# RWKV-7 steps of a hybrid decoder kernel: other PSUM rooms, other places in TensorE's queue

## The chip, the cores and the metric

The kernel runs on one core of a Trainium2 chip. The metric is device time in microseconds (us) from launch to end; less is better. Engines are named as in the profile: PE is TensorE (PEld its weight loads), DVE is VectorE, ACT is ScalarE, POOL is GpSimd, SP is SyncE, which here only issues DMAs.

## What is computed

Two decoder layers over 512 tokens of width 1024, all in float32. Each layer runs three mixers side by side on `x`, adds them behind sigmoid gates, and ends with a squared-relu MLP:

```python
proj = x @ w_in[l]
z_a, q_b, k_b, v_b, g_b, u_c, gate_logits = jnp.split(proj, PROJ_SPLITS, axis=-1)
y_a = _rwkv7_mixer(_token_shift(z_a, a_shift[l]), ...)
y_b = _retention_mixer(q_b, k_b, v_b, g_b)
y_c = _s5_mixer(u_c, ...)
gate_a, gate_b, gate_c = jnp.split(jax.nn.sigmoid(gate_logits + b_gate[l]), 3, axis=-1)
merged = gate_a * (y_a @ wb_a) + gate_b * (y_b @ wb_b) + gate_c * (y_c @ wb_c)
x = _layer_norm(DN_ALPHA * x + merged @ w_out[l], ...)
x = _layer_norm(DN_ALPHA * x + jnp.square(jax.nn.relu(x @ w_ff1[l])) @ w_ff2[l], ...)
```

The change touches the RWKV-7 mixer (`y_a`), a recurrence over tokens with a 64x64 state per head, which the kernel does in chunks of 64 tokens:

```python
def step(state, inp):
    r_t, w_t, k_t, v_t, na_t, nb_t = inp
    sa = jnp.einsum('bhvk,bhk->bhv', state, na_t)
    state = (state * w_t[:, :, None, :] + sa[..., None] * nb_t[:, :, None, :]
             + v_t[..., None] * k_t[:, :, None, :])
    return state, jnp.einsum('bhvk,bhk->bhv', state, r_t)
```

## The kernel before

A large product is split in three float32r products (`mm3`, L168 to L171: high by high, low by high, high by low), so nearly all of PE's work stands in L169 to L171. Weight blocks come by DMA (`raw`), ACT makes the high part `wh` (L151) and DVE or POOL the low part `wl` (L155); in the part that the change touches it is always DVE. `raw`, `wh` and `wl` have three buffers each.

In each layer this part is the function `weave`. It mixes nine generators into one program. The **filler** is large products: gate tiles (`gates`), the projections of four retention heads (`b_gemm`), the last gate tiles, and then the three branch products (`branch`, in the order S5, retention, RWKV). The **chains** are small steps that depend on one another: one for each of four pairs of RWKV heads (`a_pair`), one for each of four retention heads (`b_head`). A generator yields (work, latency): `weave` advances a clock by the work, and lets the chain go on when the latency has passed on that clock; until then it takes a piece of filler. At the end all PE instructions of the weave are tied into exactly that order. So a latency in a `yield` decides how much filler stands on PE between a step and the step that needs its result. The order on DVE, ACT and SP is set by the framework's scheduler; every engine works its queue in order.

A pair goes through `a_prep` (decays, key norm, the chunk matrices; transpositions at L697, L741, L763, products at L706, L731, L771), `a_inv` (a triangular inverse on POOL, in and out through DRAM), and `a_post`: a first transposition of the inverted blocks on DVE (L814, `T1` from `PD`; the traces name the tile `T`), then block products of the inverse on PE (L823, L830, L844, L854), the products of L867 and L878, the recurrence over eight chunks (L898 and L901 on PE, with the state scaled to `sbd` on DVE at L906 between them), and a tail: ACT copies the output (`oc`, L911), DVE and ACT normalise it (L918 to L925), PE transposes it (L929), and L931 to L935 apply weight, bias and the gate product L934. A retention head has its scores at L1018, its output at L1038, a norm behind it (L1042 to L1053, with a square root on ACT at L1048), and a transposition at L1061; its gates are a tanh at L999 and a product at L1000 that end a gate tile of the filler.

PSUM has eight rooms of 128x512, in four tags of two: `g` (filler), `m`, `p` and `b`. A new tile of a tag waits until the tile two before it has been read. `a_prep` takes `m`. `a_post` gets its rooms from the argument `bank`, which is `self.mps`, so `m` too; only the recurrence's output `po` is in `p`. The recurrence of pair p waits for the one of pair p-1 by the flag `chain`, but the steps ahead of it do not: they run between the recurrence steps of pair p-1.

Of the kernel before, what the change touches and what calls it, by code (L numbers as in the profile page):

```python
# [21 lines left out]
EARLY, HEAD = 8, 18.0  # L22
# [58 lines left out]
class Hybrid:  # L81
# [469 lines left out]
    def weave(self, chains, filler, head):  # L551

        insts = self.nc.cur_bb.bb.instructions
        start = len(insts)
        self.clock, self.flags, self.joined = 0.0, set(), None
        ready = {id(g): head for g in chains}
        waits = {}
        chains = list(chains)  # L560
        while chains:
            for g in chains:
                if waits.get(id(g), self.flags) is not self.flags and waits[id(g)] not in self.flags:
                    continue
                if ready[id(g)] <= self.clock:
                    break
            else:
                g = filler
                if waits.get(id(g), self.flags) is not self.flags and waits[id(g)] not in self.flags:
                    self.clock += 0.5  # L570
                    continue
            r = next(g, None)
            if r is None:
                if g is filler:
                    live = [ready[id(c)] for c in chains if id(c) not in waits or waits[id(c)] in self.flags]
                    self.clock = max(self.clock, min(live))
                else:
                    chains.remove(g)
                continue
            if isinstance(r, str):  # L580
                waits[id(g)] = r
                if g is filler and r not in self.flags:
                    self.clock += 0.5
                continue
            waits.pop(id(g), None)
            self.clock += r[0]
            ready[id(g)] = self.clock + r[1]
        for _ in filler:
            pass
        last = None  # L590
        for ins in list(insts[start:]):
            if ins.engine == mybir.EngineType.PE:
                if last is not None:
                    self.after(ins, last)
                last = ins
# [46 lines left out]
    def a_prep(self, pool, keep, p):  # L642

        nc, par = self.nc, self.par
# [42 lines left out]
        for t in range(4):  # L687
            PE.matmul(ps[:, 2 * t:2 * t + 2], lhsT=kk[:, 128 * t:128 * t + 128], rhs=self.K[:, K_BO:K_BO + 128:64],
                      start=True, stop=True)
        yield 0.4, 8.5  # L690
        ss = self.small([128, 8], "agm", 2)
        V.tensor_scalar(ss, ps[:, 0:8], 1e-24, None, op0=ALU.max)
        self.rsqrt(rn, ss)
# [1 line left out]
        ps = self.mps()  # L695
        for t in range(4):
            PE.transpose(ps[:, 128 * t:128 * t + 128], m[:, 128 * t:128 * t + 128], self.ident)  # L697
        yield 0.45, 9.0
        V.scalar_tensor_tensor(kk, k, col(P_KK), ps, op0=MUL, op1=MUL)
        V.tensor_scalar(m, a, col(P_KA), self.oka[:, p:p + 1], op0=MUL, op1=ADD)  # L700
        V.tensor_tensor(k, k, m, op=MUL)
# [22 lines left out]
        for g in range(2):  # L724
            ps = [self.mps().rearrange("p (c n) -> p c n", c=4) for _ in range(2)]
            for i in range(4):
                c = 2 * i + g
                for h in range(2):
                    rhs = RAV[H[h], c, :].rearrange("p (s i) -> p s i", i=64)
                    rhs = rhs[:, 0:2, :] if h == 0 else rhs[:, 0:3:2, :]  # L730
                    PE.matmul(ps[h][:, i, :].rearrange("p (s i) -> p s i", i=64), lhsT=BK[H[h], c, :], rhs=rhs,  # L731
                              start=True, stop=True)
            for h in range(2):
                for o, dst in ((0, AB[:, h, g:8:2, 64 * g:64 * g + 64]), (64, AA[:, h, g:8:2, :])):
                    V.tensor_tensor(dst, ps[h][:, :, o:o + 64],
                                    self.K[:, K_MA + o:K_MA + o + 64].unsqueeze(1).to_broadcast([128, 4, 64]), op=MUL)
            yield 1.1, 2.4
        ps = [self.mps().rearrange("p (c n) -> p c n", c=8) for _ in range(2)]
        for c in range(8):
            for h in range(2):  # L740
# [1 line left out]
        for h in range(2):  # L742
            S.copy(out=AB[:, h].rearrange("p (t c) n -> p t (c n)", c=2)[:, :, 64:192],
                   in_=ps[h].rearrange("p (t c) n -> p t (c n)", c=2))
        yield 0.7, 0.8
        nsc = self.dram.tile([16, 2, 64, 64], F32, name=self.nm("nsc"))
        for h in range(2):
            for q in range(2):
# [14 lines left out]
                PE.transpose(ps[h][:, c, :], RAV[H[h], c, 64:192], I64[H[h], :])  # L763
        for h in range(2):
            S.copy(out=AVX[:, h], in_=ps[h])
        yield 0.7, 2.5
        ps = self.mps().rearrange("p (c n) -> p c n", c=8)
        for c in range(8):
            for h in range(2):
# [27 lines left out]
    def a_post(self, pool, p, bank):  # L797
        nc, par = self.nc, self.par
# [3 lines left out]
        H = (slice(0, 64), slice(64, 128))  # L802
        I64 = self.K[:, K_I64:K_I64 + 64]
        tsc, AD, AJ, AB, AVX, RT, vb, pc = (self.ah[p][n] for n in ("tsc", "AD", "AJ", "AB", "AVX", "RT", "vb", "pc"))
        v = page("avb")
        nc.sync.dma_start(out=v, in_=vb)
        PD, T1 = page("PD", 1, (128, 8, 32)), page("T1", 1, (128, 8, 32))
# [4 lines left out]
                                  in_=tsc[b, 8 * h:8 * h + 8].rearrange("c j r -> j c r"))  # L812

        V.transpose(T1, PD)  # L814
        if self.joined:
            self.after(self.nc.cur_bb.bb.instructions[-1], self.joined)
        Pt = page("Pt", 1, (128, 8, 64))
        Y = T1
        Q = [slice(32 * b, 32 * b + 32) for b in range(4)]
# [3 lines left out]
                PE.matmul(ps[Q[b], c, :], lhsT=AD[Q[b], c, :], rhs=T1[Q[b], c, :], start=True, stop=True,  # L823
                          tile_position=(32 * b, 32 * b))
        V.tensor_copy(T1, ps[:, 0:8, :])
        yield 0.7, 2.8
        ps = bank().rearrange("p (c n) -> p c n", c=16)
        for c in range(8):
            for b in range(4):
# [43 lines left out]
        for g in range(2):  # L873
            cs4 = slice(4 * g, 4 * g + 4)
            ps = bank().rearrange("p (c n) -> p c n", c=4)
            for i in range(4):
                for h in range(2):
                    PE.matmul(ps[H[h], i, :], lhsT=WM[H[h], 4 * g + i, :], rhs=AB[H[h], h, 4 * g + i, :],  # L878
                              start=True, stop=True)

            blocks = lambda t: t.rearrange("p (t c) (s n) -> p t (c s) n", c=2, n=64)
            V.tensor_tensor(blocks(GM[:, cs4])[:, :, 0:4:3], blocks(ps)[:, :, 0:4:3],
                            RT[:, cs4, :].rearrange("p (t c) n -> p t c n", c=2), op=ADD)
            V.tensor_tensor(blocks(GM[:, cs4])[:, :, 1:3], blocks(ps)[:, :, 1:3],
                            I64.unsqueeze(1).unsqueeze(1).to_broadcast([128, 2, 2, 64]), op=ADD)
            evac = nc.cur_bb.bb.instructions[-1]
            yield 0.9, 0.5 + 3.5 * g
        self.joined = evac
        self.flags.add("join%d" % p)
        if p:  # L890
            yield "chain%d" % (p - 1)

        po = [self.pps().rearrange("p (t h d) -> p t h d", t=4, h=2) for _ in range(2)]
        st = None
        for c in range(8):
            ps = po[c % 2][:, c // 2]
            for h in range(2):
                PE.matmul(ps[:, h, :], lhsT=AB[:, h, c, :], rhs=AVX[:, h, c, :], start=h == 0, stop=c == 0,  # L898
                          skip_group_check=True)
            if c:  # L900
                PE.matmul(ps, lhsT=GM[:, c, :], rhs=st, start=False, stop=True, skip_group_check=True)  # L901
            if c < 7:
                st = self.sbd[2 * (p % 2) + c % 2]
                with self.ahead(-1500000):
                    for h in range(2):
                        V.tensor_scalar(st[H[h], h], ps[H[1 - c % 2], h, :], pc[H[h], c:c + 1], None, op0=MUL)  # L906
                self.joined = nc.cur_bb.bb.instructions[-1]
            yield 0.65, 1.4 if c < 7 else 1.0
        oc, o2 = AVX[:, 2], RT
        for g in range(2):  # L910
            S.copy(out=oc[H[g]], in_=po[g][H[g]].rearrange("p t h d -> p (t h) d"))  # L911
        self.flags.add("chain%d" % p)
        yield 0.0, 12.0
        if p:
            yield "done%d" % (p - 1)

# [27 lines left out]
    def a_pair(self, pool, keep, p):  # L944
        if p:
            yield "prep%d" % (p - 1)
        yield from self.a_prep(pool, keep, p)
        yield 0.4, 0.0
        self.flags.add("prep%d" % p)
        self.a_inv(keep, p)  # L950
        self.inverted = max(self.clock + 6.0, self.inverted + 1.0) + 14.0
        yield 0.0, self.inverted + 16.0 - self.clock
        if p:
            yield "join%d" % (p - 1)
        yield from self.a_post(keep, p, self.mps)


    def b_gemm(self, pool, gp, h):
# [189 lines left out]
    def layer(self, l):  # L1148
        tc, nc, a = self.tc, self.nc, self.a
# [16 lines left out]
        with ExitStack() as left:  # L1166
            with P("zpool", "right") as zp:
                gates, inner = ExitStack(), ExitStack()
                gp = gates.enter_context(P("gpool", "right"))
# [18 lines left out]
                acc, self.accs = [], []  # L1188

                def filler():  # L1190
                    yield from self.gates(gp, EARLY, 22)
                    for h in range(4):
                        yield from self.b_gemm(bp, gp, h)
                    br, y = None, None
                    last = 8 * (24 - 22) - 1
                    for i, step in enumerate(self.gates(gp, 22, 24)):
                        if br is None and ({"prep3", "head3"} <= self.flags or i == last):
                            if i == last:
                                yield "prep3"
                                yield "head3"  # L1200
                            aprep.close()
                            bpool.close()
                            br = self.br = inner.enter_context(P("br", "right"))
                            y = self.branch_in(br, 4, self.ycs, 0.25)
                        yield step
# [133 lines left out]
```

## Time and profile before

| | |
|---|---|
| time, median of 3 runs | 2178.96 us (2177.87 to 2186.68) |
| the profiled execution's own time | 2176.58 us |
| its span | 2174.8 us |
| PE busy | 2095.7 us, 96% of the span |
| DVE, ACT, POOL busy | 1183.7, 756.6, 343.3 us (54%, 35%, 16%) |
| mean granted clock of PE | 0.979 of full speed |
| chain that ended last | PE 80%, DVE 10%, DMA 4%, issue 2% |

The span is one execution between its first and last instruction; launch and end lie around it (1.8 us here). The weave lies between about 225 and 666 us in the first layer, and 1305 and 1741 us in the second. Busy PE time is modelled at the ends of matmuls, so idle time, and who ended it, says more than the busy share.

### The profile page before, as it was taken

The numbers are of one execution on the slowest core, as the hardware profiler recorded it, in microseconds if no ns is written. First come the engines' busy times: TensorE is split into PE (matmuls) and PEld (weight loads), VectorE is DVE, ScalarE is ACT, GpSimd is POOL, SyncE is SP. The second block draws the span as 40 slices with busy tenths as digits, with TensorE's granted clock in tenths as the row PEclk, the third lists the DMA queues.
The fourth block names the chain that finished last, engine by engine and source line by source line (L and its number), as shares of the span: only waits on it lengthen the run. The fifth ranks groups of instructions, "written<-read, shape, count | busy, mean of one in ns | idle before, by whom it ended". The sixth has DMA issues, their size and how long they took to land.

```text
span 2174.8 us, 31728 instructions
## 1 busy us (share of the span) xinstructions
PE 2095.7 (96%) x12784; PEld 1728.8 (79%) x12784; DVE 1183.7 (54%) x1966; ACT 756.6 (35%) x1087; POOL 343.3 (16%) x384
## 2 busy tenths in 40 slices
PE   8999999989999999999999999999899999999998
PEld 7788777768778888888887887777787878888886
DVE  7753456656556633233596534676666566243344
ACT  5423433432523333133244234334334223232231
POOL 1311021110000222112213110212200011122220
PEclk9999999989999999999999899999999999999999
DMA  9484652222365333233364856522225553232331
GB/s 227 140 141 146 185 135 77 67 79 71 121 191 198 97 115 99 78 97 106 98 160 145 131 156 178 137 82 58 79 80 163 182 184 105 80 116 78 107 107 58
DMA packets 365170, 263.95 MB, mean 121 GB/s; under 512 B 79328, under 2 KB 309856, under 8 KB 364896
## 3 DMA queue, kind: packets, MB, share of 16 engines
q1 hardware_dynamic: 365024, 261.93, 43.0%
q8 instruction: 100, 1.64, 0.3%
q14 instruction: 46, 0.38, 0.1%
HBM read 218.89 MB, written 42.99 MB: 120 GB/s over the span
## 4 chain that ended last, share of the span: by engine, by line
PE 80%; DVE 10%; DMA 4%; issue 2%; ACT 1%; POOL 1%; SPq 1%; DVEq 0%; ACTq 0%; POOLq 0%
PE g L169 23%; PE g L170 22%; PE g L171 22%; DVE wl L155 2%; PE b L1018 1%; DMA raw<-in_w_out 1%; DMA yl<-ybs 1%; PE p L898 1%; PE b L1038 1%; PE m L867 1%; PE b L171 1%; PE b L170 1%; PE b L169 1%; PE m L731 1%; PE b L490 1%
## 5 line engine op out<-in xcount | busy, mean ns | idle before, releaser
L151 ACT CAST wh<-raw 128x1024 fp32r<-128x1024 f32 x312 | 326.9, 1050 | 815.7 <-PE g L170 380.5
L169 PE MATMUL g<-xh,wh 128*128 128x512 f32 (+1 forms) x1472 | 576.7, 392 | 7.2 <-ACT wh L151 3.0
L170 PE MATMUL g<-xl,wh 128*128 128x512 f32 (+1 forms) x1472 | 564.6, 384 | 0.1
L171 PE MATMUL g<-xh,wl 128*128 128x512 f32 (+1 forms) x1472 | 564.7, 384 | 0.0
L155 DVE TENSOR_TENSOR wl<-raw,wh 128x1024 fp32r<-128x1024 f32 x230 | 297.6, 1294 | 268.6 <-ACT wh L151 266.6
L155 POOL TENSOR_TENSOR wl<-raw,wh 128x1024 fp32r<-128x1024 f32 x82 | 203.7, 2487 | 1118.5 <-ACT wh L151 1083.1
L169 PEld LDWEIGHTS g<-xh,wh 128*128 128x128 f32 x1472 | 279.2, 190 | 66.4 <-issue 8.0
L171 PEld LDWEIGHTS g<-xh,wl 128*128 128x128 f32 x1472 | 279.2, 190 | 54.6 <-issue 1.0
L170 PEld LDWEIGHTS g<-xl,wh 128*128 128x128 f32 x1472 | 279.8, 190 | 52.6 <-issue 3.0
L170 PE MATMUL g<-wl,hh 128*128 128x512 f32 x512 | 201.3, 393 | 0.0
L171 PE MATMUL g<-wh,hl 128*128 128x512 f32 x512 | 201.1, 393 | 0.0
L169 PE MATMUL g<-wh,hh 128*128 128x512 f32 x512 | 199.0, 392 | 0.0
L791 POOL TENSOR_TENSOR TLt<-NL,TL 128x120 f32<-128x120 f32 (+14 forms) x120 | 41.4, 345 | 491.1 <-DMA NL<-nsc 317.1
L170 PEld LDWEIGHTS g<-wl,hh 128*128 128x128 f32 x512 | 96.2, 188 | 22.2
L169 PEld LDWEIGHTS g<-wh,hh 128*128 128x128 f32 x512 | 96.2, 188 | 22.0
L171 PEld LDWEIGHTS g<-wh,hl 128*128 128x128 f32 x512 | 96.2, 188 | 21.4
L169 PE MATMUL g<-yh,wh 128*128 128x512 f32 x256 | 101.2, 395 | 8.1 <-ACT yh L179 5.5
L170 PE MATMUL g<-yl,wh 128*128 128x512 f32 x256 | 100.1, 391 | 0.9 <-DVE yl L177 0.5
L1273 DVE SCALAR_TENSOR_TENSOR fr<-g,fr 128x512 f32<-128x512 f32 x62 | 42.6, 687 | 106.6 <-ACT fr L1270 106.6
L171 PE MATMUL g<-yh,wl 128*128 128x512 f32 x256 | 99.7, 389 | 0.0
L1281 DVE TENSOR_TENSOR yb<-yb,g 128x512 f32<-128x512 f32 x48 | 32.8, 684 | 120.1 <-PE g L171 120.1
L177 DVE TENSOR_TENSOR hl<-fr,hh 128x512 fp32r<-128x512 f32 x64 | 68.9, 1079 | 34.4 <-ACT hh L176 34.4
(348 smaller groups left out, 2945.6 us busy)
## 6 DMA issues: line engine op xcount, KB each, us to landing
raw<-in_w_in SPq DMA_DIRECT2D x132, 512.0 KB, 4.3
raw<-in_w_ff SPq DMA_DIRECT2D x128, 512.0 KB, 4.0
raw<-in_w_branch SPq DMA_DIRECT2D x32, 512.0 KB, 4.3
gs<-gth SPq DMA_DIRECT2D x48, 256.0 KB, 2.3
gth<-gs SPq DMA_DIRECT2D x48, 256.0 KB, 3.4
raw<-in_w_out SPq DMA_DIRECT2D x16, 512.0 KB, 5.9
zs<-az SPq DMA_DIRECT2D x24, 256.0 KB, 4.2
s5tt<-gsc SPq DMA_DIRECT2D x16, 256.0 KB, 11.9
```

The source lines that it names most:

```text
L151: nc.scalar.copy(out=wh, in_=raw)
L155: eng.tensor_tensor(wl, raw, wh.bitcast(F32), op=SUB)
L169: mm(out, lhsT=wh, rhs=xh, start=first, stop=False)
L170: mm(out, lhsT=wh, rhs=xl, start=False, stop=False)
L171: mm(out, lhsT=wl, rhs=xh, start=False, stop=last)
L177: nc.vector.tensor_tensor(lo, src, hi.bitcast(F32), op=SUB)
L490: PE.matmul(yp[g][:, 64 * i:64 * i + 64], lhsT=ca, rhs=x[part][H[g], i, :], start=i == 0 and part == 0, stop=False, skip_group_check=True)
L731: PE.matmul(ps[h][:, i, :].rearrange("p (s i) -> p s i", i=64), lhsT=BK[H[h], c, :], rhs=rhs, start=True, stop=True)
L791: G.tensor_tensor(tmp[:, :, 0:n], NL[:, s:s + 1, s + 1:16].to_broadcast([128, 8, n]), TL[:, :, s:s + 1].to_broadcast([128, 8, n]), op=MUL)
L867: PE.matmul(ps[H[h], i, :].rearrange("p (s i) -> p s i", i=64), lhsT=Pt[H[h], 4 * g + i, :], rhs=AVX[H[h], h:3:2 - h, 4 * g + i, :], start ...
L1273: V.scalar_tensor_tensor(r, ps, 0.0, r, op0=ALU.max, op1=MUL)
L1281: V.tensor_tensor(y[t][:, s], y[t][:, s], ps, op=ADD)
```

## The change

Five edits.

1. `a_pair` hands `self.pps` to `a_post`: its steps take the two `p` rooms, as the recurrence does, and no longer the `m` rooms of `a_prep`.
2. The wait for `chain` of pair p-1 moves from ahead of the recurrence to the start of `a_post`: no step of pair p behind the inverse stands on PE before the last recurrence step of pair p-1.
3. The first transposition (now L818) is tied behind the last 24 DVE instructions that the program had written before; it was tied behind one (`joined`).
4. Latencies are longer: 8.5 to 10 and 9 to 10 in the key norm, 2.4 to 3.5 behind L731, 0.8 to 1.5 behind L741, 2.5 to 3.2 behind L763, 2.8 to 3.5 behind the first block product, 1.4 to 2.0 in the recurrence, 12 to 16 ahead of its tail, 16 to 18 behind the inverse.
5. Five gate tiles, not two, stand behind the retention heads in the filler. The inputs of the S5 and the retention branch are loaded at the first step among them that finds the last pair prepared and the last head done.

```diff
@@ -687,7 +687,7 @@
-        yield 0.4, 8.5
+        yield 0.4, 10.0
...
@@ -734,7 +734,7 @@
-            yield 1.1, 2.4
+            yield 1.1, 3.5
...
@@ -802,6 +802,10 @@
+        if p:
+            yield "chain%d" % (p - 1)
+
+        order = [i for i in nc.cur_bb.bb.instructions if i.engine == mybir.EngineType.DVE]
         v = page("avb")
...
         V.transpose(T1, PD)
-        if self.joined:
-            self.after(self.nc.cur_bb.bb.instructions[-1], self.joined)
+        ins = nc.cur_bb.bb.instructions[-1]
+        for i in order[-24:]:
+            self.after(ins, i)
...
         self.flags.add("join%d" % p)
-        if p:
-            yield "chain%d" % (p - 1)
...
-            yield 0.65, 1.4 if c < 7 else 1.0
+            yield 0.65, 2.0 if c < 7 else 1.0
...
-        yield 0.0, 12.0
+        yield 0.0, 16.0
...
-        yield 0.0, self.inverted + 16.0 - self.clock
+        yield 0.0, self.inverted + 18.0 - self.clock
         if p:
             yield "join%d" % (p - 1)
-        yield from self.a_post(keep, p, self.mps)
+        yield from self.a_post(keep, p, self.pps)
...
-                    yield from self.gates(gp, EARLY, 22)
+                    yield from self.gates(gp, EARLY, 19)
...
-                    last = 8 * (24 - 22) - 1
-                    for i, step in enumerate(self.gates(gp, 22, 24)):
+                    last = 8 * (24 - 19) - 1
+                    for i, step in enumerate(self.gates(gp, 19, 24)):
```

Three places show what moved. The first is DVE's queue around the first transposition of pair 0 in the first layer, before. `BK`, `av`, `bq` and `wl` belong to pair 1, to a retention head and to weight blocks.

```order
L716 TENSOR_TENSOR BK_2492<-ak_2486,aPi_2498 64x8x64 x2
L814 STREAM_TRANSPOSE T_473_2822<-PD_2821 128x256
L715 TENSOR_TENSOR BK_2492<-aa_2497,aPi_2498 64x8x64 x2
L155 TENSOR_TENSOR wl_2772<-raw_2768,wh_2770 128x1024
L707 TENSOR_TENSOR av_2487<-m_2679,av_2487 128x512
```

The same transposition in the changed kernel. It stands behind the norm of head 0 (`bnb`), a weight block and the gate product `bg_2903` of that head, which reads the tile `g_2825` of the filler.

```order
L1049 RECIPROCAL brs_2880<-brs_2880 128x4
L735 TENSOR_TENSOR AB_2864<-m_2867,kconst 128x4x64
L735 TENSOR_TENSOR AA_2865<-m_2867,kconst 128x4x64
L1050 TENSOR_TENSOR brs_2880<-brs_2880,kconst 128x4
L1051 SCALAR_TENSOR_TENSOR bnb_2881<-bmv_2841,brs_2880 128x4
L155 TENSOR_TENSOR wl_3292<-raw_3288,wh_3290 128x1024
L1000 SCALAR_TENSOR_TENSOR bg_2903<-bg_2903,g_2825 128x512
L818 STREAM_TRANSPOSE T_491_2919<-PD_2918 128x256
L830 COPY T_491_2919<-p_2931 128x256
```

It was ahead of work that did not concern it, and is now behind the end of a head. The second place is DVE's queue at the first transposition of pair 1 in the changed kernel; `sbd`, `agm` and `AVX` are the recurrence and the tail of pair 0, `bg_3652` a gate of head 1.

```order
L907 TENSOR_SCALAR sbd_698<-p_3473,apc_2050 64x64 x2
L918 TENSOR_REDUCE agm_3916<-AVX_2431 128x8
L919 TENSOR_SCALAR agm_3916<-agm_3916 128x8
L155 TENSOR_TENSOR wl_3859<-raw_3855,wh_3857 128x1024
L920 TENSOR_TENSOR AVX_2431<-AVX_2431,agm_3916 128x512
L1000 SCALAR_TENSOR_TENSOR bg_3652<-bg_3652,g_3619 128x512
L818 STREAM_TRANSPOSE T_598_3670<-PD_3669 128x256
```

It stood between two state updates of pair 0 before; now every state update and the start of the tail of pair 0 are ahead of it. The third place is PE's queue at the same point of the changed kernel, from the last recurrence step of pair 0 to the first block product of pair 1 (L828, which reads what L818 writes).

```order
L902 MATMUL p_3474<-sbd_698,GM_3308 128x128
L169 MATMUL g_3619<-xh_84,wh_3615 128x512
L170 MATMUL g_3619<-xl_85,wh_3615 128x512
L171 MATMUL g_3619<-xh_84,wl_3617 128x512
L169 MATMUL g_3661<-xh_84,wh_3657 128x512
L170 MATMUL g_3661<-xl_85,wh_3657 128x512
L171 MATMUL g_3661<-xh_84,wl_3659 128x512
L828 MATMUL p_3682<-T_598_3670,AD_3080 32x32 x32
```

Six matmuls of filler stand between the two. Before, this product stood between recurrence steps of pair 0.

## Rows read from the trace of the kernel before

**Rows 1.** The page, busy time by engine.

```profile
PE 2095.7 (96%) x12784; PEld 1728.8 (79%) x12784; DVE 1183.7 (54%) x1966; ACT 756.6 (35%) x1087; POOL 343.3 (16%) x384
```

**Rows 2.** Stretches: us; busy PE, PEld, DVE, ACT, POOL; granted clock, DMA share, GB/s.

```profile
740.00:1095.00 355.00, 354.11 (x1626) 293.77 (x1625) 139.21 (x158) 105.63 (x137) 78.79 (x38) 1.00 0.33 101
225.00:666.00 441.00, 415.80 (x3209) 339.01 (x3208) 264.37 (x534) 164.88 (x257) 44.56 (x120) 0.97 0.40 115
1305.00:1741.00 436.00, 414.28 (x3238) 338.00 (x3237) 266.55 (x534) 167.30 (x257) 46.52 (x120) 0.99 0.41 119
```

**Rows 3.** PE's waits, first layer's weave: total us, times, longest.

```profile
PE m L929 <- DVE AVX L925: 3.8, 1, 3.8
PE m L763 <- DVE Pt L835: 3.5, 2, 1.7
PE m L823 <- DVE AA L735: 2.9, 2, 2.2
PE g L169 <- ACT yh L179: 2.8, 1, 2.8
PE m L823 <- DVE T L814: 2.1, 2, 1.6
PE p L901 <- DVE sbd L906: 1.2, 2, 0.9
```

**Rows 4.** PE's waits, second layer's weave.

```profile
PE m L929 <- DVE AVX L925: 3.0, 1, 3.0
```

**Rows 5.** Stretches as in rows 2: two of low clock, one with a wait.

```profile
310.00:340.00 30.00, 25.35 (x324) 20.70 (x325) 14.81 (x31) 8.41 (x18) 9.31 (x30) 0.77 0.34 79
450.00:490.00 40.00, 32.20 (x357) 25.37 (x356) 20.15 (x39) 12.13 (x22) 7.12 (x21) 0.79 0.33 90
590.00:600.00 10.00, 6.99 (x29) 4.87 (x27) 7.32 (x11) 8.35 (x14) 0.00 (x0) 1.00 1.04 362
```

**Rows 6.** Timeline, DVE and ACT behind head 0's norm: start, us, engine, work.

```profile
365.46 0.16 DVE L1051 SCALAR_TENSOR_TENSOR bnb<-bmv,brs 128x4 f32<-128x4 f32 x1
365.65 1.93 ACT L1053 ACTIVATE bon<-b,bnb,brs 128x256 f32<-128x256 f32 x4 [1.66 <-DVE bnb L1051]
368.36 1.05 ACT L151 CAST wh<-raw 128x1024 fp32r<-128x1024 f32 x1 [0.78 <-ACT bon L1053]
369.43 1.28 ACT L999 ACT_TABLE_LOAD   x1
370.72 0.60 ACT L999 ACTIVATE bg<-g 128x512 f32<-128x512 f32 x1
371.35 0.69 DVE L1000 SCALAR_TENSOR_TENSOR bg<-bg,g 128x512 f32<-128x512 f32 x1
```

**Rows 7.** Timeline, PE: two matmuls of filler in a row, and L731.

```profile
231.25 0.39 PE L171 MATMUL g<-xh,wl 128*128 128x512 f32 x1
231.48 0.40 PE L169 MATMUL g<-xh,wh 128*128 128x512 f32 x1
...
308.80 1.16 PE L731 MATMUL m<-RAV,BK 64*128 64x128 f32 x16
```

**Rows 8.** Groups by line, DVE and ACT, 225 to 745 us: busy, mean ns | idle before.

```profile
L155 DVE TENSOR_TENSOR wl<-raw,wh 128x1024 fp32r<-128x1024 f32 x57 | 70.7, 1240 | 41.2 <-ACT wh L151 40.2 <-DMA TL<-in_kconst 0.6 <-PE b L1061 0.2
L935 DVE TENSOR_TENSOR RT<-RT,m 128x512 f32<-128x512 f32 x4 | 2.7, 686 | 0.6 <-PE m L934 0.3
L918 DVE TENSOR_REDUCE agm<-AVX 128x8 f32<-128x512 f32 x4 | 2.7, 676 | 3.0 <-ACT AVX L911 2.9
L735 DVE TENSOR_TENSOR AA<-m,kconst 128x256 f32<-128x256 f32 x16 | 6.6, 416 | 0.0
L814 DVE STREAM_TRANSPOSE T<-PD 128x256 f32<-128x256 f32 x4 | 1.8, 445 | 5.5 <-DMA PD<-tsc 4.3 <-DMA TL<-in_kconst 1.1
L911 ACT COPY AVX<-p 64x512 f32<-64x512 f32 x8 | 4.7, 581 | 16.6 <-PE m L830 7.8 <-DVE sbd L906 5.1 <-PE p L901 3.6
L931 ACT ACTIVATE RT<-m,par 128x512 f32<-128x512 f32 x4 | 3.1, 777 | 8.7 <-PE m L929 8.7
```

More of the change, by code (lines that the diff above doesn't have):

```diff
@@ L556, in weave @@
         start = len(insts)
-        self.clock, self.flags, self.joined = 0.0, set(), None
+        self.clock, self.flags = 0.0, set()
         ready = {id(g): head for g in chains}
@@ L697, in a_prep @@
             PE.transpose(ps[:, 128 * t:128 * t + 128], m[:, 128 * t:128 * t + 128], self.ident)
-        yield 0.45, 9.0
+        yield 0.45, 10.0
         V.scalar_tensor_tensor(kk, k, col(P_KK), ps, op0=MUL, op1=MUL)
@@ L744, in a_prep @@
                    in_=ps[h].rearrange("p (t c) n -> p t (c n)", c=2))
-        yield 0.7, 0.8
+        yield 0.7, 1.5
         nsc = self.dram.tile([16, 2, 64, 64], F32, name=self.nm("nsc"))
@@ L765, in a_prep @@
             S.copy(out=AVX[:, h], in_=ps[h])
-        yield 0.7, 2.5
+        yield 0.7, 3.2
         ps = self.mps().rearrange("p (c n) -> p c n", c=8)
@@ L825, in a_post @@
         V.tensor_copy(T1, ps[:, 0:8, :])
-        yield 0.7, 2.8
+        yield 0.7, 3.5
         ps = bank().rearrange("p (c n) -> p c n", c=16)
@@ L885, in a_post @@
                             I64.unsqueeze(1).unsqueeze(1).to_broadcast([128, 2, 2, 64]), op=ADD)
-            evac = nc.cur_bb.bb.instructions[-1]
             yield 0.9, 0.5 + 3.5 * g
-        self.joined = evac
         self.flags.add("join%d" % p)
-        if p:
-            yield "chain%d" % (p - 1)
         po = [self.pps().rearrange("p (t h d) -> p t h d", t=4, h=2) for _ in range(2)]
@@ L906, in a_post @@
                         V.tensor_scalar(st[H[h], h], ps[H[1 - c % 2], h, :], pc[H[h], c:c + 1], None, op0=MUL)
-                self.joined = nc.cur_bb.bb.instructions[-1]
-            yield 0.65, 1.4 if c < 7 else 1.0
+            yield 0.65, 2.0 if c < 7 else 1.0
         oc, o2 = AVX[:, 2], RT
```

## The prediction

> **What bounds the kernel now.** I read the page first, then stretches, PE's waits, and only then single places. The page says that PE is busy for 96% of the span [rows 1], so all that any reordering can win is idle time of PE, and time that PE spends at its lower clock. The stretches say where that is: 355 us of plain MLP leave PE idle for 0.9 us at full clock, the weave of the first layer for 441.0 - 415.8 = 25.2 us, that of the second for 436.0 - 414.3 = 21.7 us [rows 2]. The clock granted there averages 0.97 and 0.99; PE has two levels, 1.2 and 2.4 GHz, so the share below 1 is work lost: about 0.03 x 441 = 13 and 0.01 x 436 = 4 us. The largest piece lies in two stretches of the first layer, 30 x 0.23 = 6.9 and 40 x 0.21 = 8.4 us [rows 5]; both hold waits of PE. So some 47 us of waits and 17 us of low clock are at stake, 3% of the time.
>
> Who is waited for [rows 3]: L763 for DVE at L835, 1.7 us each time, though it reads nothing of that: it waits for a PSUM room of tag m that L835 has to empty. L823, the first block product of a pair, 2.9 + 2.1 us, for rooms and for its transposition. L929, a pair's tail, 3.8 us once (3.0 in the second layer [rows 4]), because DVE was not through with the norm. The first matmul of the S5 branch, 2.8 us for its input. The other waits of the first layer, 25.2 - 15.1 = 10 us, are some fifteen of under 2.2 us each.
>
> **The change, part by part.** No arithmetic is added; the same matmuls come in another order. So each part is a wait that goes, or a wait that comes.
>
> *What goes.* With the steps behind the inverse in the p rooms, L763 shares its rooms with L741 alone, which ACT copies two steps earlier: 3.5 us per layer, gone. The room part of L823 and the small ones of L706, L731 and L878 have the same cause and go too. The tail's latency of 16 instead of 12 moves L929 about 4 us of filler later, as much as the one long wait was: 3.8 and 3.0 us, gone. Five gate tiles behind the heads mean that the branch inputs are asked for some 20 us ahead of their first use (24 matmuls a tile at 0.23 us [rows 7], over nearly four tiles): 2.8 us per layer, gone. The loads have that stretch to land in; if they do not, L828 of pair 3 pays, because ACT copies that pair's predecessor out behind five splits of loaded tiles.
>
> *What comes: the first transposition.* L818 now stands behind the last 24 DVE instructions written before it, and whatever those wait for, it waits for. Right behind it in PE's queue stands L828 with all of the filler behind that. The price of each:
>
> Pair 0. PE issues the output product of head 0, then L731 (1.1 us) and 15 matmuls of filler (15 x 0.23 = 3.5) [rows 7], then L828: 4.6 us. DVE in the same time has four evacuations of 0.42 us [rows 8], seven smaller instructions (1.4 us, an estimate from that) and the root on ACT in between, so 3.1 us to the end of the norm. Then comes what the trace shows once at full length: from `bnb` at 365.46 us over four outputs, a cast, a table load and a tanh on ACT to the end of the gate product at 372.04 us, 6.6 us, of which 0.8 was idle [rows 6]. I take 6.0, then 0.45 for the transposition [rows 8]: 9.6 us. Wait: 5.0 us. Ends: 4.2 if the norm is done sooner, 6.6 if ACT's idle time returns and the handovers add up.
>
> Pair 1. From the last recurrence step of pair 0: ACT's copy 0.58, then on DVE L918 0.68, L919 0.2, a weight block 1.24, two passes like L935 0.69 each, transposition 0.45 [rows 8], 4.5 us, with handovers 4.9. PE has six matmuls, 1.4 us. Wait: 3.5 us, between 3.0 and 5.
>
> Pair 2. L929, L934 and L828 stand in a row. ACT needs 0.78 us for L931, DVE 0.69 for each of L932 and L935, and 0.45 [rows 8]: 2.6, with handovers 2.9, against L934, about as long as L731 [rows 7]. Wait: 1.8 us.
>
> Pair 3. Behind it stand one state update and loaded tiles; PE has its six matmuls. Wait: 0.3 us, at most 3 if the loads are late.
>
> Together 10.6 us per layer, against the 5.0 of L823 [rows 3]. This part costs 5.6 us a layer.
>
> *What stays or is shifted.* With the pairs one after another, a pair's recurrence now meets the next pair's preparation: the first state updates of pair 0 stand on DVE behind two weight blocks (1.24 us each [rows 8]), those of pair 1 behind a decay that waits for a table load. I allow 3 us per layer where 1.2 stood [rows 3]; nothing and 5 are the ends. Another 1.5 us of small waits remain, at the start of the retention branch above all.
>
> *Idle time, summed.* 10.6 + 3.0 + 1.5 = 15.1 us per layer. Gain 25.2 - 15.1 = 10.1 and 21.7 - 15.1 = 6.6: 16.7 us.
>
> *Switches.* The order of the whole program has 22 more places where PE goes from filler to small steps or back. A switch shows no wait of its own; below nothing is excluded, since more instructions are started cold, and a whole filling matmul (0.23 us) is the upper bound: 0 to 5 us, taken as 3.
>
> *Clock.* 17 us are lost now. All of it may stay, all may go. The two stretches that lose most [rows 5] hold a cluster of waits, and the stretch with the single 2.8 us wait of the branch ran at full clock [rows 5]. The clusters go, two longer single waits per layer come. I take half: 9 us gained; the ends are 0 and 17.
>
> By a rule of the Trainium skill ("TensorE: Matmul & The Clock Gate", the section on HAM oscillation) it is the long gaps of PE that throw its clock to the lower level, which then costs again after the gap. The single wait of 590 to 600 us with its clock of 1.00 does not bear it out at 2.8 us, and no row here shows one of 5. By that rule the clock term would be a loss, the third case below; by the row it stays a gain.
>
> *Sum.* 16.7 - 3 + 9 = 23 us from the profiled execution's 2176.6 gives 2154. The median of the runs shown lies 2.4 us above that execution, so I forecast **2156 us**.
>
> **The rivals.** A difference under about 0.5%, 11 us, can hardly be told from none here.
>
> *The transpositions cost no more than before.* If DVE and ACT are through sooner than I read from their queues, the four waits come to about 2 us per layer, and all of the clock returns. For it: the p rooms really are free, and DVE is busy for just 60% of the weave [rows 2]. Against it: the gate product behind the table load is ahead of L818 in the queue, and no idle DVE shortens it. 2156 - 2 x 8.6 - 8 = 2131 us.
>
> *The long waits take the clock along.* Two waits of 3.5 and 5 us per layer, each followed by a stretch like those of rows 5 that loses some 7.5 us: 4 x 7.5 = 30 us lost, 13 more than now, where I have 9 less. 2156 + 22 = 2178 us: the waits won are given back by the clock. For it: 450 to 490 us, behind the 3.8 us wait, is just that. Against it: the same wait in the second layer, 3.0 us, left that weave at 0.99 [rows 2, 4].
>
> *L828 becomes the bound, and the kernel slower.* Every L828 then pays what I expect at pair 0 at its upper end, 6.6 us, because each finds the end of a head, a tail or a late load in front of L818: 4 x 6.6 + 4.5 = 31 us idle per layer, 6 and 9 more than now, the clock as it is, the switches 3: 2179 + 18 = 2197 us. It decides from about 17 us for the four waits together in a layer: there the idle time equals today's. Against it: pair 2 and pair 3 have no head in front of them.
>
> **How the numbers follow.** Forecast 0.50, cheap transpositions 0.14, clock 0.22, slower 0.14. The forecast's own ends, from pairs 0 and 1, the recurrence and half of the clock bounds, are 2142 and 2171. To hold 8 in 10, the range takes in the cheap case below and the clock case above and leaves out the slow one: 2130 to 2180. Faster by over 0.5% (under 2168): nearly all of the forecast, all of the cheap case, a fifth of the clock case, 0.66. Within it: 0.20. Slower: most of the slow case and a tail of the clock case, 0.14.
>
> **What would show it.** Right: in PE's waits of each weave L828 for L818 or DVE heads the list with about 10 us in four, the longest near 5; L763, L929 and the branch start are gone or under 0.5; idle PE near 15 us per weave; a mean clock of 0.98 or 0.99. The DVE timeline before L818 of pair 0 would show L1000 behind a table load. Wrong: L828 under 3 us in all (cheap case), a clock under 0.97 in both weaves (clock case), or L828 over 17 us per layer (slow case). A wait at the start of the RWKV branch, or of L902 over 5 us per layer, would be a term that I have not seen.

## The result, and the profile after

The changed kernel takes 2143.81 us (median of 4 runs, 2141.71 to 2144.45) against 2178.41 us (2172.29 to 2186.68) of the kernel before beside it: ratio 0.9837, 95% interval 0.9804 to 0.9871. That is 1.6% faster, clear of the noise, inside the range, and 12 us below the 2156 forecast. The profiled execution has 2144.45 us, a span of 2142.7 and a mean clock of 0.981.

The page, busy time by engine, as in [rows 1]; then the stretches of the two weaves, as in [rows 2] (busy PE, PEld, DVE, ACT, POOL; granted clock, DMA share, GB/s):

```profile
PE 2082.1 (97%) x12784; PEld 1719.7 (80%) x12784; DVE 1182.7 (55%) x1966; ACT 744.7 (35%) x1079; POOL 349.7 (16%) x384
```

```profile
225.00:645.00 420.00, 405.91 (x3210) 332.13 (x3209) 262.39 (x533) 160.95 (x255) 48.90 (x120) 0.98 0.42 121
1285.00:1710.00 425.00, 410.94 (x3244) 336.41 (x3243) 265.91 (x535) 162.87 (x254) 48.44 (x120) 0.99 0.43 123
```

The weaves give 21 and 11 us. Idle PE falls from 25.2 to 14.1 and from 21.7 to 14.1 us, together 18.7; busy PE, for nearly the same matmuls, falls by 9.9 and 3.3. PE's waits in the first layer's weave, to be held against [rows 3]:

```profile
PE p L828 <- DVE T L818: 9.9, 3, 4.1
PE g L169 <- DVE bg L1000: 1.7, 1, 1.7
PE p L934 <- DVE Pt L863: 1.1, 1, 1.1
PE p L902 <- DVE sbd L907: 1.0, 1, 1.0
```

Of [rows 3] and [rows 4] two waits are left: the recurrence, and that of the first block product for its transposition (L823 before, L828 now), which has grown from 2.1 to 9.9 us and is two thirds of the idle time that is left. Pair 0's wait, in rows of the three engines (start, length, engine, operation; in brackets the idle time ahead and its releaser):

```profile
323.85 0.16 DVE L1051 SCALAR_TENSOR_TENSOR bnb<-bmv,brs 128x4 f32<-128x4 f32 x1
...
328.85 0.69 DVE L1000 SCALAR_TENSOR_TENSOR bg<-bg,g 128x512 f32<-128x512 f32 x1 [0.68 <-ACT bg L999]
329.45 0.44 DVE L818 STREAM_TRANSPOSE T<-PD 128x256 f32<-128x256 f32 x1
```

```profile
324.04 1.93 ACT L1053 ACTIVATE bon<-b,bnb,brs 128x256 f32<-128x256 f32 x4 [1.36 <-DVE bnb L1051]
325.85 1.05 ACT L151 CAST wh<-raw 128x1024 fp32r<-128x1024 f32 x1
326.92 1.28 ACT L999 ACT_TABLE_LOAD   x1
328.22 0.60 ACT L999 ACTIVATE bg<-g 128x512 f32<-128x512 f32 x1
```

```profile
325.47 0.39 PE L171 MATMUL g<-xh,wl 128*128 128x512 f32 x1
329.94 1.08 PE L828 MATMUL p<-T,AD 32*32 32x32 f32 x64 [4.09 <-DVE T L818]
```

From `bnb` to the transposition lies the chain of the prediction: four outputs, a cast, a table load, a tanh, the gate product. Pairs 1 and 2 wait 3.38 and 2.43 us, pair 3 not at all; the second layer repeats it (4.09, 3.38, 2.44). What follows each wait stands in stretches of 10 us (busy PE, clock, DMA share, GB/s):

```profile
320.00:330.00 10.00, 5.91 (x41) 0.97 0.05 13
330.00:340.00 10.00, 10.00 (x177) 0.69 0.43 99
390.00:400.00 10.00, 6.62 (x91) 0.88 0.37 106
400.00:410.00 10.00, 10.00 (x101) 0.78 0.00 1
480.00:490.00 10.00, 7.57 (x111) 0.83 0.57 183
```

### The profile page after: what moved, and what is told of

Same layout as the page of the kernel before. It is cut to its first block, busy times and chain, and to the rows that moved or that the text cites. A ratio compares the mean times of both kernels' runs of the same rounds, so it can differ in the third digit from the quotient of the medians.

```text
span 2142.7 us, 31702 instructions
## 1 busy us (share of the span) xinstructions
PE 2082.1 (97%) x12784; PEld 1719.7 (80%) x12784; DVE 1182.7 (55%) x1966; ACT 744.7 (35%) x1079; POOL 349.7 (16%) x384
## 4 chain that ended last, share of the span: by engine, by line
PE 89%; DVE 7%; issue 1%; ACT 1%; DMA 1%; SPq 0%; DVEq 0%; ACTq 0%
PE g L169 25%; PE g L170 25%; PE g L171 24%; PE b L1038 1%; DVE wl L155 1%; PE p L899 1%; PE m L731 1%; PE b L1018 1%; PE p L883 1%; PE p L872 1%; PE b L171 1%; PE b L170 1%; PE b L169 1%; PE p L902 1%; PE b L495 1%
## 5 line engine op out<-in xcount | busy, mean ns | idle before, releaser
L169 PE MATMUL g<-xh,wh 128*128 128x512 f32 (+1 forms) x1472 | 580.1, 395 | 10.6 <-DVE bg L1000 3.4
L171 PE MATMUL g<-xh,wl 128*128 128x512 f32 (+1 forms) x1472 | 567.2, 386 | 0.0
L169 PEld LDWEIGHTS g<-xh,wh 128*128 128x128 f32 x1472 | 281.2, 191 | 71.5 <-issue 7.0
L171 PEld LDWEIGHTS g<-xh,wl 128*128 128x128 f32 x1472 | 281.3, 191 | 55.1 <-issue 1.0
L171 PE MATMUL g<-wh,hl 128*128 128x512 f32 x512 | 201.1, 393 | 0.0
L169 PE MATMUL g<-wh,hh 128*128 128x512 f32 x512 | 199.0, 392 | 0.0
L791 POOL TENSOR_TENSOR TLt<-NL,TL 128x120 f32<-128x120 f32 (+14 forms) x120 | 49.5, 413 | 536.4 <-DMA NL<-nsc 527.7
L169 PEld LDWEIGHTS g<-wh,hh 128*128 128x128 f32 x512 | 96.2, 188 | 22.0
L171 PEld LDWEIGHTS g<-wh,hl 128*128 128x128 f32 x512 | 96.1, 188 | 21.5
L169 PE MATMUL g<-yh,wh 128*128 128x512 f32 x256 | 104.1, 407 | 0.0
L171 PE MATMUL g<-yh,wl 128*128 128x512 f32 x256 | 100.0, 391 | 0.0
L1281 DVE TENSOR_TENSOR yb<-yb,g 128x512 f32<-128x512 f32 x48 | 32.8, 684 | 120.5 <-PE g L171 120.5
## 6 DMA issues: line engine op xcount, KB each, us to landing
s5tt<-gsc SPq DMA_DIRECT2D x16, 256.0 KB, 12.7
```

The costliest lines, as they stand in the source:

```text
L169: mm(out, lhsT=wh, rhs=xh, start=first, stop=False)
L171: mm(out, lhsT=wl, rhs=xh, start=False, stop=last)
L791: G.tensor_tensor(tmp[:, :, 0:n], NL[:, s:s + 1, s + 1:16].to_broadcast([128, 8, n]), TL[:, :, s:s + 1].to_broadcast([128, 8, n]), op=MUL)
L1281: V.tensor_tensor(y[t][:, s], y[t][:, s], ps, op=ADD)
```

## The experiments

My theory from this: each edit removes its own stops, and the tie of edit 3 costs most of what is still lost. The rivals were that the latencies did it all, or that the tie is harmless. All runs at a glance; old tie means behind one instruction, cover means 4.5 us of other work between the first transposition and its reader, and the last column is how long VectorE stood at the first transposition (eight of them) until its pieces had landed. Idle is span less busy PE of the profiled execution, which is one of the runs and not always near the median: 2169.6 us for the latencies alone, 2210.0 for the tiles alone, 2151.7 for three tiles. Edits 1 and 2 were never tried apart, so what "rooms" gives stands for both.

| rooms (1, 2) | tie (3) | latencies (4) | gate tiles (5) | median us | ratio, 95% interval | idle, busy PE | VectorE stood |
|---|---|---|---|---|---|---|---|
| no | old | old | 2 | 2180 (before) | 1 | 79.1, 2095.7 | 7.7 |
| no | old | old | 5 | 2215.28 | 1.0149 (1.0124 to 1.0173) | 102.6, 2105.7 | 12.2 |
| yes | old | old | 2 | 2133.66 | 0.9784 (0.9757 to 0.9810) | 55.7, 2083.2 | 9.5 |
| no | old | new | 2 | 2179.15 | 0.9992 (0.9974 to 1.0011) | 79.3, 2088.5 | 32.4 |
| yes | old | new | 2 | 2150.68 | 0.9870 (0.9848 to 0.9893) | 65.8, 2083.5 | 31.3 |
| yes | old | old | 5 | 2171.15 | 0.9962 (0.9948 to 0.9977) | 77.2, 2094.6 | 13.8 |
| no | old | new | 5 | 2168.65 | 0.9947 (0.9928 to 0.9965) | 77.4, 2088.7 | 27.0 |
| yes | old | new | 5 | 2118.14 | 0.9717 (0.9693 to 0.9741) | 43.0, 2072.9 | 12.7 |
| yes | old | new | 3 | 2146.61 | 0.9853 (0.9834 to 0.9872) | 62.2, 2087.7 | 14.7 |
| yes | none | new | 5 | 2152.62 | 0.9877 (0.9858 to 0.9896) | 60.5, 2089.2 | 55.6 |
| yes | last 24 | new | 5 | 2143.81 (the change) | 0.9837 (0.9804 to 0.9871) | 60.6, 2082.1 | 0 |
| yes | 18 of 24 | new | 5 | 2110.99 | 0.9693 (0.9668 to 0.9719) | 40.9, 2069.2 | 0 |
| yes | last 24, cover | new | 5 | 2107.03 | 0.9673 (0.9648 to 0.9699) | 36.3, 2070.7 | 0 |
| yes | 18 of 24, cover | new | 5 | 2106.84 | 0.9670 (0.9652 to 0.9688) | 37.0, 2067.6 | 0 |

### Five gate tiles alone

```diff
-                    yield from self.gates(gp, EARLY, 22)
+                    yield from self.gates(gp, EARLY, 19)
```

(and the two lines below it that name 22, as in the change).

> The kernel before with five gate tiles kept for the end of a weave instead of two, nothing else. Theory (each edit removes its own stops): the first products of the branch no longer wait for yh, yl and mg (4.5 us idle in layer 1 and 3.6 in layer 2 at L169 in the kernel before, most of it 2.8 behind L179), all else stays, so the time falls by 7 to 9 us, to about 2170. Rival (the late tiles only move the wait to the weave's end): within 2 us of before.

Both missed: 35 us slower. The branch's waits did shrink, to 1.1 and 0.5 us per program, but L706 now waits for `ao` (10.4 us in all) and L901 for the state updates (18.4). VectorE and TensorE at L706:

```profile
301.10 0.45 DVE L814 STREAM_TRANSPOSE T<-PD 128x256 f32<-128x256 f32 x1 [5.69 <-DMA TL<-in_kconst]
301.47 1.18 DVE L155 TENSOR_TENSOR wl<-raw,wh 128x1024 fp32r<-128x1024 f32 x1
302.57 0.74 DVE L704 SCALAR_TENSOR_TENSOR ao<-ar,par,ak 128x512 f32<-128x512 f32 x1
```

```profile
303.46 2.05 PE L706 MATMUL m<-ao,kconst 128*128 128x512 f32 x2 [3.44 <-DVE ao L704]
```

VectorE stands 5.69 us at the transposition until a transfer lands, and L704, which has nothing to do with it, stands behind. The transfer named is another one, but in the trace the last piece of `PD` lands at 300.93 us, 0.2 us before the transposition starts. In the kernel before, L704 ran at 294.52, ahead of the transposition. The three tiles moved to the end had shifted the rest against it.

### The rooms alone

```diff
-        yield from self.a_post(keep, p, self.mps)
+        yield from self.a_post(keep, p, self.pps)
```

(and the wait for `chain` at the head of `a_post`).

> The kernel before with the steps behind the inverse in the recurrence's rooms and the wait for the previous pair's recurrence at their head; old latencies, old tie of the first transposition, two gate tiles. Theory (shared rooms made the waits): the waits of L763 for the copy behind L835 (3.5 us a layer), of the first block product for the masks (2.9), and those of L731, L706 and L878 (0.8 to 0.9 each) go, L929 keeps its 3.8 and 3.0; with the half clock and the products' own length that follow each stop, 20 to 25 us faster, about 2156. Rival (the latencies did it; the rooms alone only trade one wait for another, since the recurrence itself takes two rooms of the same set): at most 8 us faster, 2170 or more, with waits of similar length on other lines.

The theory's side, and more than it: 46 us, better than the whole change. TensorE's waits, whole program:

```profile
PE p L901 <- DVE sbd L906: 9.2, 8, 2.4
PE m L731 <- DVE AA L735: 6.7, 4, 3.3
...
PE m L763 <- ACT AB L743: 3.1, 6, 1.4
```

The waits for L835 and L884 are gone, and so are those of L823 and L878 for the masks; L731's own wait for them has grown. L763 is not quite free: it waits for ScalarE's copy of its own rooms, 3.1 us where 6.9 stood. L929's wait is gone too, with the old latency of 12.

### The longer latencies alone

```diff
-            yield 1.1, 2.4
+            yield 1.1, 3.5
```

(and the other eight).

> The kernel before with the nine longer latencies alone. Theory (shared rooms made most waits): only L929's wait (3.8 and 3.0 us) and the short ones behind L731 and in the recurrence go, the waits for rooms stay in some form; 6 to 12 us faster, about 2169. Rival (the latencies are the whole change, since a wait for a room is only a step that was put too early): 20 us faster or more, 2158 or less.

No change at all, so both missed. L929's wait went, as expected, and a stop of 6.8 and 6.3 us in the two layers came: L169 for `bsw` at L971. Its cause shows two experiments further on.

### The change with the old tie

```diff
...
-        ins = nc.cur_bb.bb.instructions[-1]
-        for i in order[-24:]:
-            self.after(ins, i)
+        if self.joined:
+            self.after(nc.cur_bb.bb.instructions[-1], self.joined)
...
+                self.joined = nc.cur_bb.bb.instructions[-1]
```

> The changed kernel with the first transposition tied behind the recurrence's last state update again, as before. Theory (the tie behind the last 24 instructions of VectorE makes the 9.9 us that the first block product waits in each layer, since they hold a gate's product which waits for a filler product just ahead): that wait falls to 2 to 4 us a layer, the half clock behind it goes too, and the time falls by 15 to 20 us, to about 2126. Rival (the tie is harmless: the transposition is late because VectorE's queue is full there, and further ahead it would hold up the queue until its pieces have landed): within 4 us of the changed kernel, or slower, with stops on other lines.

The theory holds, with more than the 15 to 20 us that it said: L828 does not wait at all, every stretch of 10 us in both weaves has full clock, and edit 3 by itself costs 2143.8 - 2118.1 = 26 us in this company. The old tie has a price too: VectorE stands at the transposition, with little harm here. The only stop of TensorE close behind is that of L1018 for a head's `bs`, 0.9 and 1.6 us.

```profile
L818 DVE STREAM_TRANSPOSE T<-PD x8: 445/445/446, 302.6 to 1582.7; 128x256 f32<-128x256 f32 x8
its engine sat idle before it (us, times) until:
  DMA PD<-tsc: 6.7, 1
  DMA TL<-in_kconst: 6.0, 1
```

### That kernel without the five tiles

The gate tiles of the kernel above set back to two.

> Rooms and longer latencies, the old tie of the first transposition, two gate tiles at the end: the fastest kernel so far (2118.1 us) without the five tiles. Theory (the five tiles cover the branch's first products, whose wait is 3.6 to 4.5 us a layer in the kernel before): that wait comes back, 6 to 9 us slower, about 2126. Rival (the tiles are a loss in themselves, as they were alone, 35 us): faster than 2118, 2105 or less.

Both missed: 32.5 us slower. The stop of the latencies alone is back (6.8 and 5.4 us), and its rows on VectorE and TensorE tell where it comes from:

```profile
294.38 1.22 DVE L155 TENSOR_TENSOR wl<-raw,wh 128x1024 fp32r<-128x1024 f32 x1 [1.63 <-ACT wh L151]
306.94 0.45 DVE L818 STREAM_TRANSPOSE T<-PD 128x256 f32<-128x256 f32 x1 [11.34 <-DMA gs<-gth]
...
314.22 0.69 DVE L969 TENSOR_TENSOR bq<-g,kconst 128x512 f32<-128x512 f32 x1
314.92 0.69 DVE L970 TENSOR_TENSOR bsw<-g,kconst 64x512 f32<-64x512 f32 x1
```

```profile
316.37 0.58 PE L169 MATMUL g<-wh,xh 128*128 128x256 f32 x1 [6.76 <-DVE bsw L971]
```

VectorE stands 11.34 us at the transposition, until 0.3 us after the last piece of `PD` has landed (306.65 us), and then works for 6.9 us on what has piled up. A head's swaps (L969 to L971), which empty a room of the filler, come behind that, and with them the filler itself stops. The latencies alone show the same: 11.20 us there, 6.84 us at L169.

### That kernel without the longer latencies

The nine latencies of the fastest kernel so far set back.

> Rooms and five gate tiles, the old tie, the old latencies: the fastest kernel so far (2118.1 us) without the longer latencies. Theory (what the latencies are worth shows only once the rooms are apart: the rooms alone still had L731 behind the masks 6.7 us in all, L901 behind the state updates 9.2 and L763 behind ScalarE 3.1): those waits stay, 15 to 20 us slower, about 2135. Rival (the latencies are worth nothing, as they were alone): within 4 us of 2118.

The theory's direction, three times its size: 53 us slower. VectorE stands 6.67 us at the transposition with L704 behind it, and L706 waits 4.48 us, the picture of the five tiles alone. So the latencies are worth 53 us with rooms and tiles, 47 with the tiles, 1 alone, and cost 17 with the rooms.

### Other work between the transposition and its reader

```diff
             self.after(ins, i)
+        yield 0.0, 4.5
...
-        yield 0.0, self.inverted + 18.0 - self.clock
+        yield 0.0, self.inverted + 13.5 - self.clock
```

> The changed kernel with 4.5 us of other work put between the first transposition and the block product that reads it (the steps behind the first inverse start 4.5 us earlier to make up for it). Theory (the wait of 4.1, 3.4 and 2.4 us in each layer is only a transposition issued too shortly before its reader): the waits at that product fall from 9.9 to under 1 us a layer, the half clock behind them goes, 20 to 26 us faster, 2118 to 2124. Rival (the tie keeps the transposition behind work of VectorE that comes later still, or the 4.5 us that each pair's chain becomes longer is paid elsewhere): the wait moves, 2135 or more.

The theory holds, and with 37 us gives more than the 20 to 26 that it said: L828 waits for nothing. The weaves, as in [rows 2], have next to no idle time and full clock:

```profile
225.00:635.00 410.00, 407.53 (x3247) 334.39 (x3247) 271.60 (x549) 165.24 (x260) 48.92 (x120) 1.00 0.44 127
1265.00:1680.00 415.00, 412.61 (x3271) 338.71 (x3270) 270.45 (x541) 167.29 (x259) 48.62 (x120) 1.00 0.45 129
```

Starting pair 0 earlier also makes the last 24 instructions older ones: its transposition now runs at 320.48, ahead of the gate product. Both, the cover and this, are in the number.

### The tie without the newest six instructions

```diff
-        for i in order[-24:]:
+        for i in order[-24:-6]:
```

> The changed kernel with the first transposition tied behind 18 of VectorE's last 24 instructions, the newest 6 left out. Theory (it is the newest few, a gate's product whose filler product has just run and the normalization's steps of the pair before, that make it late): the waits at the first block product fall from 9.9 us a layer to under 3, 2118 to 2126. Rival (the order on VectorE is set by when things are ready and the tie only happens to stand there, or the 18 hold late ones too): the wait keeps 6 us a layer or more, 2135 or more.

The theory holds, again with more than it said: 32.8 us faster than the change, with the order on TensorE in the weaves as it was. L828 waits 2.1 us in all where it waited 19.8, VectorE never stands at the transposition, and the stretches in which the change lost time are whole:

```profile
PE p L828 <- DVE T L818: 2.1, 2, 1.0
```

```profile
320.00:330.00 10.00, 10.00 (x183) 1.00 0.19 53
330.00:340.00 10.00, 10.00 (x128) 1.00 0.55 104
390.00:400.00 10.00, 10.00 (x139) 1.00 0.27 91
```

Of the 32.6 us between the two spans 19.7 is idle and 12.9 is busy PE.

### Latencies and tiles without the rooms

The change with edits 1 to 3 undone.

> Longer latencies and five gate tiles without the rooms: the eighth corner of the cube of those three edits under the old tie (none 2180, rooms 2133.7, latencies 2179.2, tiles 2215.3, rooms and latencies 2150.7, rooms and tiles 2171.2, all three 2118.1). Theory (shared rooms make waits of their own in any order, so the rooms are worth about 45 us here as they were against the kernel before: 46.3, 28.5 and 44.1 in the three other pairs): 2155 to 2170, with waits of L763, L823 or L731 for VectorE's copies out of rooms. Rival (the latencies and the tiles belong together and do most of it): 2130 or less.

As the theory said, in time: the rooms are worth 50.5 us here. Of the waits it named, those of L731 for copies out of rooms are there (8.0 us in all), but the largest stop was another: the filler for a gate product (L169 for L1000, 17.7 us in two). L823 for its transposition took 9.9.

### No tie

The three lines of the tie left out, the rest as in the change.

> The changed kernel with no tie on the first transposition at all: it then stands far ahead in VectorE's queue, at pair 0 between the steps of the next pair's preparation. Theory (a tie is needed, since so far ahead it waits in the queue for its pieces, and all of VectorE behind it): VectorE shows waits of several us for the transposition's pieces in the rows of the transposition, TensorE's stops move to the lines behind it (L706, L969 and the like), 2135 us or more. Rival (a tie costs in any form; the pieces have landed long before): no such waits, 2105 to 2118.

The theory's time, and its waits on VectorE, of the transposition's rows:

```profile
its engine sat idle before it (us, times) until:
  DMA TL<-in_kconst: 38.1, 5
  DMA PD<-tsc: 17.5, 3
```

But TensorE does not stop where I had said; it stops in the recurrence (L899, 13.3 us) and at the scores (L1015, 7.4). In the next two rows a state update stands behind pair 2's transposition:

```profile
461.85 0.45 DVE L818 STREAM_TRANSPOSE T<-PD 128x256 f32<-128x256 f32 x1 [6.13 <-DMA PD<-tsc]
```

```profile
462.93 0.79 PE L899 MATMUL p<-sbd,GM 128*128 128x128 f32 x2 [3.49 <-DVE sbd L904]
```

### Both cures

Cover and the tie of 18 together.

> Both cures together: 4.5 us of other work between the first transposition and its reader, and the tie behind 18 of the last 24 instructions. Theory (either of them already takes the wait away, so the second adds nothing): 2104 to 2110, within 3 us of the kernel with the cover alone (2107.0). Rival (the earlier tie also frees the gate's product that still stops TensorE 3.4 us in all with the tie of 18, or the two shift the order apart): outside that.

As the theory said: 2106.84, no second gain. This is 1.7% under the change and 3.3% under the kernel before.

### Three gate tiles

Three in place of five, with rooms, latencies and the old tie.

> Rooms, longer latencies and the old tie with three gate tiles at the end, between two (2150.7 us) and five (2118.1). With two, TensorE stops 6.8 us in one place of each layer at the products of a head (L169 behind L971), where VectorE has a head's swaps, a pair's preparation and another pair's state updates to do at once. Theory (the number of tiles sets where the heads fall against the pairs; one tile shifts the heads by some 11 us and moves them off that place at once): the 6.8 us stop goes and with it most of the difference, 2120 to 2130. Rival (the tiles give filler at the end, and each gives its share): a third of the difference, about 2140.

The 6.8 us stop went at once, as the theory had it; the time did not follow: 2146.6, less gained than either side had said. Seven other waits of the weaves come to 2.4 to 6.6 us each per program, that of L901 to less than with two tiles (10.0), the rest to more or for the first time, with VectorE standing 14.7 us:

```profile
PE p L901 <- DVE sbd L906: 6.6, 4, 2.8
```

My reason for the stop, too much work on VectorE at once, was at best the smaller part: the rows of the two-tile kernel show it standing for 11.34 us first, and working for 6.9 us behind that.

## Why the prediction held, step by step

**What goes.** L763, L823's room, the small room waits and the branch start went as said. Two causes were not as I put them. For L763 I named the rooms; they took 6.9 us to 3.1, the rest went with the longer latencies. These alone free L763 as well, but then L741 waits for the same copy (L835, 3.3 us), so only the rooms take that wait out of the program. L929's wait, which I gave to the latency of 16, is absent in every run, with rooms alone, tiles alone or latencies alone: any shift removes it, so its cause is not shown.

**What comes.** The step on which the forecast rested held: L828 was to wait 5.0, 3.5, 1.8 and 0.3 us, and waits 4.09, 3.38, 2.43 and 0; 9.9 for 10.6. Recurrence and rest were taken as 4.5 and measured 1.0 + 3.2. Idle time per layer: 15.1 forecast, 14.1 measured; gain 16.7 forecast, 18.7 measured.

**Clock.** In the profiled executions, summed over the stretches of 10 us below 0.93 in the weaves, 19.3 us were lost before and 12.6 now: a gain of 6.7 where I took 9. The size is not firm: over 17 executions of the kernel before, the mean clock goes from 0.974 (2186.88 us) to 0.981 (2171.46 us). My argument for it was weaker than its size. I held that single waits leave the clock alone, by the one wait of 2.8 us in [rows 5], and read 450 to 490 us there as a cluster. But behind its first wait, the 3.8 us of L929, the clock is 0.50 from 457.46 to 465.46 us, before any other wait; and in the changed kernel six of 2.4 to 4.1 us each stand in or ahead of a slow stretch, 12.6 / 6 = 2.1 us a wait. The clock case had the mechanism right, and with 7.5 us a wait its size wrong. The Trainium skill ("TensorE: Matmul & The Clock Gate", HAM oscillation) has the rule that long gaps of PE throw its clock down and the time after the gap pays for it. The six go that way, the 4.1 us waits above all; that waits of 2.4 us do it too is not in that section.

**Switches: the step that failed.** I charged 3 us for 22 more switches, each of which starts small steps cold. No run shows such a charge, and in the traces PE goes from filler (L169 to L171) to another line or back 433 times after and 425 before, 8 more. Instead busy PE fell by 13.6 us in the program; the clock explains 6.7, and some 7 us are left. Part of it is seen at single products: one that a wait interrupts, or that stands behind one, is recorded longer. L763 cut in two by its wait, and L934 behind and without a wait, in the second layer before; then L763 in one piece, after:

```profile
1555.14 0.27 PE L763 MATMUL m<-kconst,RAV 64*128 64x64 f32 x1
1557.14 0.69 PE L763 MATMUL m<-kconst,RAV 64*128 64x64 f32 x15 [1.73 <-DVE Pt L835]
1627.44 1.10 PE L934 MATMUL m<-az,g 128*128 128x512 f32 x2 [0.86 <-ACT RT L931]
1678.60 1.02 PE L934 MATMUL m<-az,g 128*128 128x512 f32 x2
```

```profile
434.65 0.71 PE L763 MATMUL m<-kconst,RAV 64*128 64x64 f32 x16
```

That is 0.25 and 0.08 us a wait; PE has 44 waits in the two weaves before and 15 after, and for the 29 fewer it makes 2 to 7 us, an estimate. What is left beyond that stays open. So the -3 should have been about +7, and the clock 7 instead of 9: 18.7 + 7 + 7 is, rounded, the 32 us by which the spans differ.

**The parts.** I added the edits up as if each had its price. The list of waits held for the five together; the single prices did not: under the old tie the tiles cost 35 us alone and save 33 beside rooms and latencies. Only the rooms save in any company under the old tie (28 to 51 us). Why is seen in three pairs of rows above: what a shift puts behind the standing transposition, `ao`, a head's swaps or a state update, is what TensorE then waits for. Not every stop was followed; the 18.4 us of L901 with the five tiles alone came with a VectorE that was busy, not standing. The change without its five tiles, and without its latencies, was not tried under the new tie.

## What to carry to other kernels

Where an instruction that waits for a transfer stands in an in-order queue, tie it behind work that is surely done when its reader is due and surely later than the transfer; a tie to the newest instructions hands their lateness to the reader, and no tie makes the whole queue wait. Price a stop of TensorE above its length: here 19.7 us of idle time cost 32.6. In an order set by latencies, test edits in each other's company, for their single prices do not add.

## What the runs showed that I had not expected

A wait of 2.43 us was followed by a stretch at 0.83 (480 to 490 us above), while one of 2.8 us before the change left its stretch at 1.00 [rows 5]: the length of the single wait does not decide alone. Nor does the work around it. With the latencies alone, L901 waits in both layers as long for a state update, with the same matmuls ahead of it and behind it:

```profile
379.49 0.49 PE L901 MATMUL p<-sbd,GM 128*128 128x128 f32 x2 [3.36 <-DVE sbd L906]
1455.89 0.49 PE L901 MATMUL p<-sbd,GM 128*128 128x128 f32 x2 [3.38 <-DVE sbd L906]
```

Behind the first the clock stayed at 1.00 (379.5 to 384.5 us), behind the second it was 0.66 (1455.9 to 1460.9). What decides stays open, and with it the price of a single wait.

A short product that a wait interrupts is recorded a third longer (0.96 us for 0.71 at L763).
